# Scores of head pairs in two-bank PSUM tiles, with the softmax of a pair in single VectorE instructions

## The chip, the cores and the metric

The kernel runs on one core of one Trainium2 chip. The metric is the device time of one execution in microseconds (us). Before the change the median of 3 runs is 740.6 us (740.55 to 742.78). The profiled execution took 741.12 us, of which 739.3 us is the span, from the first to the last recorded instruction.

## The reference, cut to what matters

One inference step of a small decoder with model width 1024, for a prompt of 256 tokens and for 8 sample tokens with 256 cached positions each: an S5 (state-space) layer with a gated output, a squared-ReLU MLP, an attention layer, and a second MLP, all in float32. In the attention layer every query mixes three branches with gates: a compressed one, a selection one and a window one.

```
q  = rope(rms_norm(h @ w_q));  gates = sigmoid(h @ w_gate)      # 16 query heads of 64, 4 KV heads
p_c = masked_softmax(q @ kc);  p_s = masked_softmax(q @ ks);  p_w = masked_softmax(q @ kw)
o  = g0 * (p_c @ vc) + g1 * (p_s @ vs) + g2 * (p_w @ vw)
x  = x + o @ w_o
x  = x + square(relu(rms_norm(x) @ w_up)) @ w_down
```

With 256 tokens the selection takes every causal block, and the window of 512 covers the whole prompt. So the selection and the window branch of a head are two causal softmaxes over 256 keys, with different keys and values.

## The kernel before, in words

Prompt and sample tokens stand side by side as 264 columns (NT), features on the 128 partitions. A dense product splits a float32 weight tile into a rounded part and a rest (wsplit, L590 on ScalarE and L591 on VectorE), and makes three matmuls of each pair of tiles (mm3, L597 to L599).

The stages follow each other: the S5 layer to about 133 us, its gated product and the first MLP to 364, keys, values and queries to 441, the attention to 528, the output product to 554, the second MLP to the end. The S5 stage has an order written out by hand; the code of the other stages is written as generators, and the scheduler of the framework orders the instructions of each engine by when their tiles and buffers come free. So the number of PSUM buffers behind each tag is part of what sets the order.

PSUM has 8 banks of 2 KB a partition, 512 float32 each. The tags and their buffers are set at the end of the file: PSC (whole kernel) has fl=2 and tr=3; PSA (S5, gated product, first MLP) has mm=3; PSB (from then on) has sc=2 for scores and po=1 for attention outputs, and mm stands for the two fl banks there.

The prompt attention (prompt_attn) goes through 12 units (gp, rp, u). A unit is two heads, one of each of the KV groups 2gp and 2gp+1, whose keys lie on partitions 0 to 63 and 64 to 127. With u = 0 it is the first 128 queries of two heads for each group, with u = 1 or 2 the second 128 queries of one head each. In step i the code issues the scores of unit i, the softmax of unit i-1, and the transposes and value products of unit i-2.

- scores (L1181): two tiles of tag sc, one bank each. For u > 0 a product over 64 rows gives 512 columns of a head, selection and window side by side (L1195), and a product with a triangle constant adds the causal mask (L1198). For u = 0 the mask comes first (L1187), and then L1191, 256 columns a time.
- softmax (L1202): for each bank on its own a maximum on VectorE (L1212), one exponential on ScalarE for each row of scores (L1214, 4 or 2 a bank), and on VectorE the reciprocal, the gates (L1218) and the product (L1223). P has four buffers.
- transposed (L1227) brings P into key order by four transposes a bank (L1232), and values (L1244) multiplies with the values into the one po bank.

Beside the units runs other work, in two generators, side_a and side_b. The first has the rest of the second query group (q1: dense product, transposes L934, normalisation and rotary form from L987 on, transposes back L944 and copy L945) and the compressed branch of the second pair of groups; the second is the attention of the 8 sample tokens (sample_qk, sample_attn), which takes banks of tag mm. The tables SIDE and SIDB say how many steps of each are issued behind each unit, and Q1 how many steps of q1 come before the first unit. cmp_branch(0), the compressed branch of the first pair of groups, is issued before the first scores (products L1156).

Of the kernel before, what the change touches and what calls it, by code (L numbers as in the profile page):

```python
# [81 lines left out]
F32 = mybir.dt.float32  # L82
# [75 lines left out]
def s5_stage(K, filler):  # L158
# [183 lines left out]
    def chunk_in(h):  # L342
        St[h] = e8([128, 2, 16, 73], f"St{h}")
        for ri in range(2):
            S.activation(St[h][:, ri, :, 0:8], st[:, h, ri], AF.Copy, scale=1.0 - 2 * ri)
        for q0 in range(0, 8, 3):
            n = min(3, 8 - q0)
            pt = [ps("mm"), ps("tr")]
            for q in range(n):
                qq = q0 + q  # L350
                for ri in range(2):
                    o = 146 * q + 73 * ri
                    for b in range(2):
                        for a in range(2):
                            nc.tensor.matmul(pt[a][64 * b:64 * b + 64, o:o + 73],
                                             ET[h][64 * a:64 * a + 64, qq, ri, 64 * b:64 * b + 64],
                                             U[64 * a:64 * a + 64, h, qq, b], start=True, stop=True)
            for a in range(2):
                pv_ = pt[a][:, 0:146 * n].rearrange("p (q r n) -> p r q n", r=2, n=73)
                sl = slice(2 * q0 + a, 2 * (q0 + n), 2)  # L360
                S.activation(St[h][:, :, sl, 8:73], pv_[:, :, :, 8:73], AF.Copy)
                S.activation(bu[:, h, :, sl], pv_[:, :, :, 0:8], AF.Copy)
# [163 lines left out]
    pys = {}  # L526
# [14 lines left out]
    for ft in range(4, 8):  # L541
        pys[ft] = ps("mm" if ft < 7 else "tr")
        conv(ft, pys[ft])
# [152 lines left out]
PDP = ()  # L696
PDA = ()
# [60 lines left out]
def sample_compress(K):  # L758
# [27 lines left out]
    for s in range(2):  # L786
# [3 lines left out]
        pts = [K.ps("fl"), K.ps("fl")]  # L790
# [157 lines left out]
def kv_post(K, br):  # L948
# [9 lines left out]
    pk = token_major(K, "sc", kv[:, 0:2])  # L958
# [6 lines left out]
    pv = token_major(K, "sc", kv[:, 2:4])  # L965
# [118 lines left out]
def gates(K, xh, xl):  # L1084
# [11 lines left out]
    S.activation(g, g, AF.Sigmoid)  # L1096
    K.gp = at.tile([128, 2, 16, 3], F32, name="gp")
# [44 lines left out]
def prompt_attn(K, oh, ol, side):  # L1142
# [38 lines left out]
    def scores(gp, rp, u):  # L1181

        banks = [K.ps("sc"), K.ps("sc")]
# [16 lines left out]
        return banks  # L1200

    def softmax(gp, rp, u, banks):  # L1202
        n = 4 if u == 0 else 2
        L = 512 // n
        out = []
        for g2 in range(2):
            head = (2 * gp + g2) * 4 + 2 * rp + max(u - 1, 0)
            sv = banks[g2].rearrange("p (n k) -> p n k", n=n)
            nm = aa.tile([128, n], F32, tag="nm", name="nm", bufs=6)
            den = aa.tile([128, n], F32, tag="den", name="den", bufs=6)  # L1210
            P = aa.tile([128, 522], F32, tag="P", name="P", bufs=4)[:, 0:512].rearrange("p (n k) -> p n k", n=n)
            V.tensor_reduce(nm, sv, AX.X, ALU.max, negate=True)  # L1212
            for i in range(n):
                S.activation(P[:, i], sv[:, i], AF.Exp, bias=nm[:, i:i + 1], accum_out=den[:, i:i + 1])  # L1214
            V.reciprocal(den, den)
            g = K.gp[:, 0, head:head + 2, 1:3] if u == 0 else K.gp[:, 1, head:head + 1, 1:3]
            dv = den.rearrange("p (h b) -> p h b", b=2)
            V.tensor_tensor(dv, dv, g, ALU.mult)  # L1218
            if (u > 0, g2) in PDA:
                for i in range(n):  # L1220
                    S.activation(P[:, i], P[:, i], AF.Copy, scale=den[:, i:i + 1])
            else:
                (G if (u > 0, g2) in PDP else V).tensor_tensor(P, P, den.unsqueeze(2).to_broadcast([128, n, L]), ALU.mult)  # L1223
            out.append(P)
        return out

    def transposed(gp, rp, u, Ps, PTs):  # L1227
        for g2 in range(2):
            pt = K.ps("tr")
            Pf = Ps[g2].rearrange("p n k -> p (n k)")  # L1230
# [29 lines left out]
    cmp_branch(0)  # L1260
    for i in range(n + 2):
        if i < n:
            sc[i] = scores(*units[i])
        if 1 <= i <= n:
            sm[i - 1] = softmax(*units[i - 1], sc.pop(i - 1))
# [78 lines left out]
def sample_attn(K, oh, ol):  # L1344
# [6 lines left out]
    for bh in range(2):  # L1351
        p1, p2 = K.ps("mm"), K.ps("mm")
# [53 lines left out]
        pc = K.ps("mm")  # L1406
        nc.tensor.matmul(pc[:, 0:64], ptx[:, 0], K.vcs[:, bh], start=True, stop=True)
# [5 lines left out]
        V.tensor_tensor(o, o, pc[:, 0:64], ALU.add)  # L1413
# [34 lines left out]
def build(ctx, tc, A, O):  # L1448
# [13 lines left out]
    K.ps = lambda tag: pools[tag][0].tile([128, 512], F32, tag=pools[tag][2], name="ps_" + tag, bufs=pools[tag][1])  # L1462
# [63 lines left out]
    pools["mm"] = pools["fl"]  # L1526
    with ExitStack() as es:
# [59 lines left out]
        with ExitStack() as ek:  # L1587
# [15 lines left out]
            def side(i, cmp_branch):  # L1603
                if not steps:
                    steps.extend([side_a(cmp_branch), side_b()])
                for _ in range(SIDE[i]):
                    next(steps[0], None)
                for _ in range(SIDB[i]):
                    next(steps[1], None)
            prompt_attn(K, oh, ol, side)  # L1610
            for s in steps:
                for _ in s:
                    pass
        yh, yl = ft(F32R, "yh"), ft(F32R, "yl")
# [14 lines left out]
PSC = dict(fl=2, tr=3)  # L1629
PSA = dict(mm=3)  # L1630
PSB = dict(sc=2,po=1)
SIDE = (3,1,1,1,0,0,1,1,1,1,0,0,0,0)
SIDB = (1,2,2,2,2,2,2,2,0,0,0,0,0,0)
Q1 = 2
# [95 lines left out]
```

## Time and profile before

| | |
|---|---|
| Median of the runs | 740.6 us (740.55 to 742.78) |
| Profiled execution, its own time | 741.12 us |
| Its span | 739.3 us |
| PE (TensorE) busy | 700.2 us, 95% of the span, 6,214 matmuls |
| DVE (VectorE) busy | 531.7 us, 72% |
| ACT (ScalarE) busy | 404.6 us, 55% |
| POOL (GpSimd) busy | 74.8 us, 10% |
| Mean granted clock of TensorE | 0.975 of full speed |
| Chain that ended last | PE 83%, DVE 13%, ACT 2% |

PE is the matmul side of TensorE and PEld its weight loads, which run beside the matmuls. The granted clock is the TensorE clock as a share of 2.4 GHz. Matmuls are pipelined, and the ends of their records are modelled: a record's length holds latency too, so from one matmul to the next it is the distance of their starts that counts. The chain follows the work that ended last back to what released it, step by step.

### The profile page before, as it was taken

To read this page: it belongs to the slowest core of one execution; us is meant where nothing else is said; L and a number is where in the kernel's file an instruction comes from. 1 tells how busy PE (TensorE), PEld (TensorE's weight loads), DVE (VectorE), ACT (ScalarE), POOL (GpSimd) and SP (SyncE) were. 2 spreads that over 40 slices of the span, in tenths; PEclk is the share of its full clock that TensorE was granted. 3 is DMA by queue.
4 is the path that set the end of the run, shared out by engine and by line. 5 is a ranking of instruction groups with operands and counts; after the bars stand their busy time and mean duration, and the time that the engine had idled before them with its cause. 6 is when DMAs were issued, how large, how long until landed. Compare 5 with 4: busy or idle time off the path is not lost.

```text
span 739.3 us, 16322 instructions
## 1 busy us (share of the span) xinstructions
PE 700.2 (95%) x6214; PEld 650.7 (88%) x6214; DVE 531.7 (72%) x1209; ACT 404.6 (55%) x907; POOL 74.8 (10%) x127
## 2 busy tenths in 40 slices
PE   2789897999999999999998999999999999999997
PEld 2787777999999999999988984565899999999997
DVE  7899995978777766656677868887678777755553
ACT  3463532666666655445466575657466666644442
POOL 0000623111000000000002224110020000000000
PEclk9989897999999999999999996999999999999999
DMA  7342423686767758555555564100255555556551
GB/s 263 81 158 77 161 99 118 197 289 193 229 234 262 277 175 298 186 175 188 177 175 179 188 187 142 59 3 1 86 172 182 188 173 182 189 180 201 192 190 40
DMA packets 53328, 124.70 MB, mean 169 GB/s; under 512 B 6522, under 2 KB 26874, under 8 KB 52994
## 3 DMA queue, kind: packets, MB, share of 16 engines
q1 hardware_dynamic: 51714, 121.23, 49.9%
q10 hardware_dynamic: 1536, 2.42, 0.9%
q8 instruction: 49, 0.80, 0.5%
q14 instruction: 29, 0.24, 0.1%
HBM read 120.63 MB, written 7.18 MB: 173 GB/s over the span
## 4 chain that ended last, share of the span: by engine, by line
PE 83%; DVE 13%; ACT 2%; issue 1%; DMA 1%; SPq 0%; ACTq 0%; DVEq 0%
PE ps_mm L597 23%; PE ps_mm L598 22%; PE ps_mm L599 22%; PE ps_sc L1195 3%; PE ps_tr L296 2%; PE ps_tr L1232 2%; PE ps_po L1253 2%; DVE ca L431 1%; DVE St L434 1%; DVE St L433 1%; DVE cb L432 1%; DVE St L455 1%; DMA U<-x_chunks_in 1%; DVE big L454 1%; PE ps_sc L1198 1%
## 5 line engine op out<-in xcount | busy, mean ns | idle before, releaser
L591 DVE TENSOR_TENSOR wl<-raw,wh 128x512 fp32r<-128x512 f32 x344 | 241.1, 703 | 149.5 <-ACT wh L590 146.5
L590 ACT ACTIVATE wh<-raw 128x512 fp32r<-128x512 f32 x344 | 216.0, 631 | 210.7 <-PE ps_mm L598 157.8
L597 PE MATMUL ps_mm<-hh,wh 128*128 128x264 f32 x512 | 145.3, 284 | 0.0
L598 PE MATMUL ps_mm<-hl,wh 128*128 128x264 f32 x512 | 145.0, 283 | 0.0
L599 PE MATMUL ps_mm<-hh,wl 128*128 128x264 f32 x512 | 145.0, 283 | 0.0
L598 PEld LDWEIGHTS ps_mm<-hl,wh 128*128 128x128 f32 x512 | 96.5, 188 | 0.0
L597 PEld LDWEIGHTS ps_mm<-hh,wh 128*128 128x128 f32 x512 | 96.4, 188 | 0.0
L599 PEld LDWEIGHTS ps_mm<-hh,wl 128*128 128x128 f32 x512 | 96.0, 187 | 0.0
L598 PE MATMUL ps_mm<-yl,wh 128*128 128x264 f32 x256 | 72.9, 285 | 0.0
L597 PE MATMUL ps_mm<-yh,wh 128*128 128x264 f32 x256 | 72.6, 284 | 0.0
L597 PE MATMUL ps_mm<-xh,wh 128*128 128x264 f32 x256 | 72.6, 284 | 0.0
L599 PE MATMUL ps_mm<-yh,wl 128*128 128x264 f32 x256 | 72.5, 283 | 0.0
L598 PE MATMUL ps_mm<-xl,wh 128*128 128x264 f32 x256 | 72.4, 283 | 0.0
L599 PE MATMUL ps_mm<-xh,wl 128*128 128x264 f32 x256 | 72.3, 284 | 0.0
L597 PEld LDWEIGHTS ps_mm<-yh,wh 128*128 128x128 f32 x256 | 48.2, 188 | 0.0
L598 PEld LDWEIGHTS ps_mm<-xl,wh 128*128 128x128 f32 x256 | 48.2, 188 | 0.0
L597 PEld LDWEIGHTS ps_mm<-xh,wh 128*128 128x128 f32 x256 | 48.2, 188 | 0.0
L599 PEld LDWEIGHTS ps_mm<-yh,wl 128*128 128x128 f32 x256 | 48.2, 188 | 0.0
L598 PEld LDWEIGHTS ps_mm<-yl,wh 128*128 128x128 f32 x256 | 48.1, 188 | 0.0
L599 PEld LDWEIGHTS ps_mm<-xh,wl 128*128 128x128 f32 x256 | 47.9, 188 | 0.0
L628 POOL TENSOR_TENSOR nacc<-nacc,sq 128x264 f32<-128x264 f32 x21 | 16.9, 803 | 251.9 <-ACT sq L627 251.9
L598 PE MATMUL ps_mm<-gl,wh 128*128 128x264 f32 x128 | 36.6, 289 | 0.0
(424 smaller groups left out, 1482.3 us busy)
## 6 DMA issues: line engine op xcount, KB each, us to landing
raw<-w_up_in SPq DMA_DIRECT2D x64, 512.0 KB, 3.8
raw<-w_down_in SPq DMA_DIRECT2D x64, 512.0 KB, 3.6
raw<-s_w_glu_in SPq DMA_DIRECT2D x16, 512.0 KB, 4.8
w<-cmp_w_in SPq DMA_DIRECT2D x12, 512.0 KB, 4.5
raw<-w_kv_in SPq DMA_DIRECT2D x12, 512.0 KB, 3.5
blk<-cache_cmp_in SPq DMA_DIRECT2D x64, 64.0 KB, 1.9
raw<-w_q_in SPq DMA_DIRECT2D x8, 512.0 KB, 3.7
win_old_out<-cache_win_kv_in SPq DMA_DIRECT2D x8, 510.0 KB, 5.2
```

Source lines behind the costliest of these rows:

```text
L296: nc.tensor.matmul(pm[:, 0:73], sameT, sq[:, h, q, b], start=(h + q + b == 0), stop=(h + q + b == 9))
L431: TT(a, x, m(SR), ALU.mult)
L432: TT(b_, x[:, ::-1], m(SQ), ALU.mult)
L590: nc.scalar.activation(h[:, :, cols], src[:, c:c + 4], AF.Copy)
L591: nc.vector.tensor_tensor(l[:, :, cols], src[:, c:c + 4], h[:, :, cols].bitcast(F32), ALU.subtract)
L597: nc.tensor.matmul(out, wh, xh, start=start, stop=False)
L598: nc.tensor.matmul(out, wh, xl, start=False, stop=False)
L599: nc.tensor.matmul(out, wl, xh, start=False, stop=stop)
L628: nc.gpsimd.tensor_tensor(self.acc, self.acc, sq, ALU.add)
L1195: nc.tensor.matmul(banks[g2], K.QT[hs[g2], 4 * gp + 2 * rp + u - 1, 128:256], K.KTp[hs[g2], gp], start=True, stop=False)
L1232: nc.tensor.transpose(pt[:, 128 * j:128 * j + 128], Pf[:, 128 * j:128 * j + 128], K.ident)
L1253: nc.tensor.matmul(po[64 * g2:64 * g2 + 64, 128 * kt:256], K.Vp[:, kt, br, 64 * g:64 * g + 64], rhs, start=False, stop=(br == 1 and kt == 1))
```

## The change

PSUM tiles of a new tag s2 have 1,024 columns, two banks. A unit's scores stand in one such tile, each head in one bank of it. The softmax takes the pair in one maximum, one reciprocal, one product with the gates and one product with P, which is now one tile of 1,024 columns with two buffers. The exponentials stay one to a row of scores. The eight banks are dealt anew: PSC has fl=1 and tr=2, PSA has mm=4 and a bank fb, PSB has two s2 (four banks) and po=1. In the stages after the first MLP a product of tag mm takes in turn the fl bank and half of each s2 tile; during the attention it takes the fl bank alone.

Smaller edits: the keys' and values' transposes (token_major) go to tag tr; the S5 stage names its banks anew; the samples' scores take an s2 tile, and their compressed output (pc) shares the po bank; the gates get a one-element exponential (tle) behind their sigmoid; cmp_branch(0) is issued behind the first scores; and the tables SIDE, SIDB and Q1 have new numbers.

```diff
     S.activation(g, g, AF.Sigmoid)
+    S.activation(ak.tile([1, 1], F32, name="tle"), g[0:1, 0:1], AF.Exp)
...
-        banks = [K.ps("sc"), K.ps("sc")]
+        pair = K.ps("s2")
+        banks = [pair[:, 0:512], pair[:, 512:1024]]
...
     def softmax(gp, rp, u, banks):
         n = 4 if u == 0 else 2
...
+        sv = banks.rearrange("p (n k) -> p n k", n=2 * n)
+        nm = aa.tile([128, 2 * n], F32, tag="nm", name="nm", bufs=4)
+        den = aa.tile([128, 2 * n], F32, tag="den", name="den", bufs=4)
+        P = aa.tile([128, 1024], F32, tag="P", name="P", bufs=2)
+        Pv = P.rearrange("p (n k) -> p n k", n=2 * n)
+        V.tensor_reduce(nm, sv, AX.X, ALU.max, negate=True)
+        for i in range(2 * n):
+            S.activation(Pv[:, i], sv[:, i], AF.Exp, bias=nm[:, i:i + 1], accum_out=den[:, i:i + 1])
+        V.reciprocal(den, den)
...
+        V.tensor_tensor(dv, dv, g, ALU.mult)
+        V.tensor_tensor(Pv, Pv, den.unsqueeze(2).to_broadcast([128, 2 * n, 512 // n]), ALU.mult)
+        return P[:, 0:512], P[:, 512:1024]
...
-    cmp_branch(0)
     for i in range(n + 2):
         if i < n:
             sc[i] = scores(*units[i])
+        if i == 0:
+            cmp_branch(0)
...
-        p1, p2 = K.ps("mm"), K.ps("mm")
+        pair = K.ps("s2")
+        p1, p2 = pair[:, 0:512], pair[:, 512:1024]
...
+    K.mm = ["mm"]
+
+    def ps(tag):
+
+        if tag == "mm":
+            tag = K.mm[0]
+            K.mm.append(K.mm.pop(0))
+            if tag == "s2":
+                return ps(tag)[:, 0:512]
...
-    pools["mm"] = pools["fl"]
+    wide = ["fl", "s2", "s2"]
+    K.mm = list(wide)
...
+            K.mm = ["fl"]
             prompt_attn(K, oh, ol, side)
...
+            K.mm = list(wide)
...
-PSC = dict(fl=2, tr=3)
-PSA = dict(mm=3)
-PSB = dict(sc=2,po=1)
-SIDE = (3,1,1,1,0,0,1,1,1,1,0,0,0,0)
-SIDB = (1,2,2,2,2,2,2,2,0,0,0,0,0,0)
-Q1 = 2
+PSC = dict(fl=1, tr=2)
+PSA = dict(mm=4, fb=1)
+PSB = dict(s2=2, po=1)
+SIDE = (1,1,1,2,2,2,1,1,1,1,0,0,0,0)
+SIDB = (0,0,0,1,2,2,2,2,2,2,2,0,0,0)
+Q1 = 1
```

TensorE at the start of the prompt attention, before. The names are those of the code; qr is a query tile that is brought into token order, P the probabilities of a unit:

```order
L934 MATMUL ps_mm<-ident,qr_5939 128x128 x4
L1156 MATMUL ps_po<-kcb,QT 128x16 x8
L1300 MATMUL ps_mm<-ssq,cst 128x96
L1195 MATMUL ps_sc<-KTp,QT 128x512
L1198 MATMUL ps_sc<-triR,identR 128x2x128
L1195 MATMUL ps_sc<-KTp,QT 128x512
L1198 MATMUL ps_sc<-triR,identR 128x2x128
L1195 MATMUL ps_sc<-KTp,QT 128x512
L1198 MATMUL ps_sc<-triR,identR 128x2x128
L1232 MATMUL ps_tr<-ident,P 128x128 x4
L1195 MATMUL ps_sc<-KTp,QT 128x512
L1198 MATMUL ps_sc<-triR,identR 128x2x128
```

The same place after; the scores of three units, with the tiles ps_s_5998, ps_s_6070 and ps_s_6126, and other products between them:

```order
L932 MATMUL ps_tr<-ident,kv 128x128 x4
L1099 MATMUL ps_tr<-ident,gT 128x48 x2
L1191 MATMUL ps_s_5998<-KTp,QT 128x256 x4
L1195 MATMUL ps_s_6070<-KTp,QT 128x512 x2
L1198 MATMUL ps_s_6070<-triR,identR 128x2x128 x2
L1107 MATMUL ps_tr<-cst,glt 128x3
L972 MATMUL ps_tr<-ident,kv 8x128 x2
L942 MATMUL ps_fl<-ident,qn 128x128 x4
L1107 MATMUL ps_tr<-cst,glt 128x3
L1294 MATMUL ps_fl<-ssq,cst 128x96
L1195 MATMUL ps_s_6126<-KTp,QT 128x512 x2
L1198 MATMUL ps_s_6126<-triR,identR 128x2x128 x2
```

The two products L1195 of a unit and its two masks L1198 now stand next to each other, where they alternated. Work that was done before this place (the transposes of values and gates) now stands in it.

ScalarE at the same place, before; t is the square of a query tile, P the exponentials:

```order
L987 ACTIVATE t<-ps_mm 128x512
L1298 ACTIVATE ssq<-sK 128x96
L1214 ACT_TABLE_LOAD
L1214 ACTIVATE P,den<-ps_sc,nm 128x128 x8
L1214 ACTIVATE P,den<-ps_sc,nm 128x256 x4
```

And after:

```order
L985 ACTIVATE t<-ps_fl 128x512
L943 ACTIVATE KTp<-ps_tr 128x2x256
L965 ACTIVATE tm<-ps_tr,rt 128x256 x2
L1100 ACTIVATE gp<-ps_tr 128x96
L973 ACTIVATE vnew<-ps_tr,rt 8x256
L943 ACTIVATE QT<-ps_fl 128x512
L1109 ACTIVATE gs<-ps_tr 128x6
L1292 ACTIVATE ssq<-sK 128x96
L1211 ACTIVATE P,den<-ps_s_5998,nm 128x128 x8
L1211 ACTIVATE P,den<-ps_s_6070,nm 128x256 x4
```

The table load is gone from here, and between the last square of a query tile and the first exponential stand seven evictions, among them the copy of the last query tiles (QT).

## Rows read from the trace of the kernel before

**Rows 1.** Stages: stretch, length, busy PE, PEld, DVE, ACT, POOL, clock, DMA, GB/s.

```profile
178.00:364.10 186.10, 186.10 (x1540) 186.03 (x1539) 123.39 (x220) 106.46 (x213) 6.68 (x13) 1.00 0.67 221
441.40:462.90 21.50, 19.55 (x67) 11.23 (x66) 17.47 (x63) 13.11 (x48) 8.88 (x15) 0.68 0.46 146
462.90:523.10 60.20, 60.09 (x446) 35.58 (x444) 46.55 (x148) 37.03 (x152) 5.89 (x14) 1.00 0.06 19
```

**Rows 2.** The same view, the attention's first part split by the granted clock.

```profile
441.40:446.20 4.80, 2.85 (x21) 2.38 (x20) 4.04 (x12) 4.63 (x17) 0.53 (x1) 1.00 0.89 272
446.20:459.80 13.60, 13.60 (x31) 6.74 (x30) 10.79 (x47) 6.95 (x28) 7.30 (x13) 0.50 0.42 135
```

**Rows 3.** TensorE groups, 441.4 to 528.4: count, busy, mean ns, idle before.

```profile
L1195 PE MATMUL ps_sc<-KTp,QT 64*128 64x512 f32 x32 | 21.3, 751 | 1.7 <-ACT P L1214 1.6
L1191 PE MATMUL ps_sc<-KTp,QT 64*128 64x256 f32 x24 | 6.0, 417 | 0.0
```

**Rows 4.** Timeline of TensorE: start, length of the group, instruction, records.

```profile
435.21 1.13 PE L1191 MATMUL ps_sc<-KTp,QT 64*128 64x256 f32 x8
...
461.52 1.13 PE L1191 MATMUL ps_sc<-KTp,QT 64*128 64x256 f32 x4
...
465.92 1.12 PE L1195 MATMUL ps_sc<-KTp,QT 64*128 64x512 f32 x2
466.98 0.38 PE L1198 MATMUL ps_sc<-triR,identR 128*128 128x256 f32 x1
467.29 1.12 PE L1195 MATMUL ps_sc<-KTp,QT 64*128 64x512 f32 x2
468.34 0.39 PE L1198 MATMUL ps_sc<-triR,identR 128*128 128x256 f32 x1
468.57 0.60 PE L1232 MATMUL ps_tr<-ident,P 128*128 128x128 f32 x4
```

**Rows 5.** Timeline of all engines near 443 us; idle before in brackets.

```profile
441.87 1.93 PE L1156 MATMUL ps_po<-kcb,QT 128*128 128x16 f32 x16 [0.35 <-DVE vcm L1079]
...
442.83 1.28 ACT L1214 ACT_TABLE_LOAD   x1
...
444.13 0.37 ACT L1214 ACTIVATE P<-ps_sc,nm 128x128 f32<-128x128 f32 x1
...
445.51 0.38 ACT L1214 ACTIVATE P<-ps_sc,nm 128x128 f32<-128x128 f32 x1
...
445.69 1.63 PE L1195 MATMUL ps_sc<-KTp,QT 64*128 64x512 f32 x2 [1.60 <-ACT P L1214]
```

**Rows 6.** Timeline of TensorE where the compression tail stands.

```profile
133.71 0.27 PE L823 MATMUL ps_fl<-ident,kc 128*64 128x128 f32 x1 [0.52 <-DVE kc L755]
```

**Rows 7.** Groups of the query normalisation, from 436 or 441.4 to 528.4.

```profile
L987 ACT ACTIVATE t<-ps_mm 128x512 f32<-128x512 f32 x2 | 1.2, 595 | 0.2 <-PE ps_mm L934 0.2
L988 DVE TENSOR_REDUCE ss<-t 128x8 f32<-128x512 f32 x2 | 1.3, 672 | 0.0
L991 DVE TENSOR_TENSOR qn<-ps_mm,T0q 128x512 f32<-128x512 f32 x2 | 1.4, 676 | 0.0
L993 DVE TENSOR_TENSOR t<-ps_mm,T1q 128x256 f32<-128x256 f32 x4 | 1.5, 414 | 0.0
L133 DVE TENSOR_TENSOR rs<-rs 128x8 f32<-128x8 f32 x6 | 1.3, 215 | 0.0
L998 POOL TENSOR_TENSOR qn<-qn,ri 128x512 f32<-128x512 f32 x2 | 2.6, 1301 | 9.6 <-DVE den L1218 8.8 <-DVE ri L137 0.8
L945 ACT ACTIVATE QT<-ps_mm 128x512 f32<-128x512 f32 x2 | 1.2, 600 | 0.0
```

**Rows 8.** ScalarE group, 364.1 to 441.4, eviction of a query tile.

```profile
L1124 ACT ACTIVATE qr<-ps_mm 128x264 f32<-128x264 f32 x7 | 2.6, 375 | 0.0
```

**Rows 9.** VectorE: a group of the attention, and one instruction of the timeline.

```profile
L1212 DVE TENSOR_REDUCE nm<-ps_sc 128x2 f32<-128x512 f32 x16 | 11.0, 688 | 6.7 <-PE ps_sc L1198 6.7
...
379.51 1.26 DVE L925 TENSOR_TENSOR kv<-kv,rstd 128x1056 f32<-128x1056 f32 x1 [0.59 <-ACT rstd L904]
```

More of the change, by code (lines that the diff above doesn't have):

```diff
@@ L347, in chunk_in @@
             n = min(3, 8 - q0)
-            pt = [ps("mm"), ps("tr")]
+            pt = [ps("mm"), ps("mm")]
             for q in range(n):
@@ L541, in s5_stage @@
     for ft in range(4, 8):
-        pys[ft] = ps("mm" if ft < 7 else "tr")
+        pys[ft] = ps("mm")
         conv(ft, pys[ft])
@@ L695 @@
 NP = 'm'
-PDP = ()
-PDA = ()
 CPA = (0,)
@@ L789, in sample_compress @@
         yield
-        pts = [K.ps("fl"), K.ps("fl")]
+        pts = [K.ps("fl"), K.ps("fb")]
         for lc in range(4):
@@ L957, in kv_post @@
     tm = K.ak.tile([128, 2, 512], F32, tag="tmk", name="tm", bufs=2)
-    pk = token_major(K, "sc", kv[:, 0:2])
+    pk = token_major(K, "tr", kv[:, 0:2])
     G.tensor_copy(K.sK[:, 2 * br - 2:2 * br], kv[:, 0:2, 0:8])
@@ L964, in kv_post @@
         yield
-    pv = token_major(K, "sc", kv[:, 2:4])
+    pv = token_major(K, "tr", kv[:, 2:4])
     for qt in range(2):
@@ L1199, in scores @@
                                  K.triR.unsqueeze(1).to_broadcast([128, 2, 128]), start=False, stop=True)
-        return banks
+        return pair
     def softmax(gp, rp, u, banks):
         n = 4 if u == 0 else 2
[L1204 to L1224, printed above, removed]
@@ L1225, in softmax @@
-        return out
+        sv = banks.rearrange("p (n k) -> p n k", n=2 * n)
[6 more added lines that the diff above has]
+            S.activation(Pv[:, i], sv[:, i], AF.Exp, bias=nm[:, i:i + 1], accum_out=den[:, i:i + 1])
@@ L1227, in transposed @@
+        V.reciprocal(den, den)
+        head = 8 * gp + 2 * rp + max(u - 1, 0)
+        g = K.gp[:, min(u, 1)].rearrange("p (g h) b -> p g h b", h=4)[:, 2 * gp:2 * gp + 2, head % 4:head % 4 + n // 2, 1:3]
+        dv = den.rearrange("p (g h b) -> p g h b", g=2, b=2)
+        V.tensor_tensor(dv, dv, g, ALU.mult)
+        V.tensor_tensor(Pv, Pv, den.unsqueeze(2).to_broadcast([128, 2 * n, 512 // n]), ALU.mult)
+        return P[:, 0:512], P[:, 512:1024]
     def transposed(gp, rp, u, Ps, PTs):
@@ L1229, in transposed @@
             pt = K.ps("tr")
-            Pf = Ps[g2].rearrange("p n k -> p (n k)")
+            Pf = Ps[g2]
             for j in range(4):
@@ L1405, in sample_attn @@
                                      vr[bh][br][:, b4, pg], start=False, stop=(br == 1 and pg == 1))
-        pc = K.ps("mm")
-        nc.tensor.matmul(pc[:, 0:64], ptx[:, 0], K.vcs[:, bh], start=True, stop=True)
+        pc = po[:, 256:320]
+        nc.tensor.matmul(pc, ptx[:, 0], K.vcs[:, bh], start=True, stop=True)
         t = K.tmp.tile([128, NT], F32, tag="t", name="so")[:, 0:256].rearrange("p (g d) -> p g d", g=4)
@@ L1412, in sample_attn @@
         V.tensor_reduce(o, t.rearrange("p g d -> p d g"), AX.X, ALU.add)
-        V.tensor_tensor(o, o, pc[:, 0:64], ALU.add)
+        V.tensor_tensor(o, o, pc, ALU.add)
         yield
@@ L1461, in psum @@
             pools[tag] = pool, bufs[tag], tag
-    K.ps = lambda tag: pools[tag][0].tile([128, 512], F32, tag=pools[tag][2], name="ps_" + tag, bufs=pools[tag][1])
+    K.mm = ["mm"]
[5 more added lines that the diff above has]
+                return ps(tag)[:, 0:512]
+        pool, bufs, t = pools[tag]
+        return pool.tile([128, 1024 if tag == "s2" else 512], F32, tag=t, name="ps_" + tag, bufs=bufs)
+    K.ps = ps
     psum(ctx, "pc", PSC)
```

## The prediction

> **What bounds the kernel now.** I read the stages first (busy time by stretch), then the chain of waits, then the TensorE rows of the attention, then the waits inside it. In the dense stages TensorE is busy all the time: 1,540 matmuls start in 186.1 us, one every 0.12 us, at the full clock [rows 1]. Nothing but fewer matmuls shortens those, and the change removes none; more PSUM buffers there are worth nothing. The prompt attention, from 441.4 to about 528 us, is the other kind of stage: TensorE is busy 60.09 of 60.2 us in its second part, but not by work that has to take so long, and in its first part 13.6 us run at a granted clock of 0.50, the 1.2 GHz level [rows 1, 2]. DVE is busy 46.55 and ScalarE 37.03 of the same 60.2 us, so both come behind TensorE. What a change of TensorE's order in this stage gains is therefore real until DVE or a wait takes over.
>
> **The change part by part.** All sums go against the profiled execution: span 739.3, its own time 741.1 us. The 1.8 us around the span stay. The median of the runs is 740.6, so 0.5 us come off at the end.
>
> *Scores in pairs.* A unit is two heads of two KV groups. Its two score matmuls use rows 0 to 63 and rows 64 to 127 of the array. Before, the banks came free one at a time, and the scheduler put the causal mask (L1198) of the first between them. After, all 8 units with u > 0 issue L1195 twice in a row, then L1198 twice. What the neighbourhood is worth, the trace shows on L1191, the same product for u = 0: eight records on both halves, in turn, take 1.13 us (435.21), and four records on one half take 1.13 us too (461.52) [rows 4]. The two halves run side by side. One L1195 alone holds TensorE 1.05 us (465.92 to 466.98, 467.29 to 468.34; 32 records, 16 matmuls [rows 3, 4]). So 8 units x 1.05 = 8.4 us. Of the four units with u = 0, two are in pairs already; the unit at gp 1 becomes one, 1.06, and the one at rp 1 half, since eight transposes stand in its middle, 0.5 (24 records of L1191 in the stretch [rows 3]): 1.6 us. Each change between the two forms also costs: L1198 before L1195 takes 0.31 us (466.98 to 467.29), before a transpose 0.23 (468.34 to 468.57), so 0.09 rounded up [rows 4]; two changes less per unit, 8 x 2 x 0.09 = 1.4. Together 11.4 us at the full clock. Bounds: 1.4 if two 512-column products do not overlap, 11.4 if they do; I take 11.4, because the nearest row is the same line of work at 256 columns.
>
> *Waits that go.* TensorE waits 1.60 us at 445.69 for the first exponentials, which stood behind a table load of 1.28 us on ScalarE [rows 5]. The new one-element exponential in the gates loads that table earlier, under dense products: 1.6 us go. The compression tail moves out of the first dense stage into the MLP, and with it the 0.52 us at 133.71 [rows 6]; if its new place waits as long, that is nought.
>
> *Waits that come.* First, the pipeline's start. Two units' scores are issued, and the third needs the first pair of banks, which is released by all 8 exponentials of the first unit. In ScalarE's new order they stand behind the copy of QT, which needs the whole normalisation of the second query group: 0.60 (L987) + 0.67 + 0.68 + 2 x 0.41 on DVE + two small ones of 0.2 each + eleven rsqrt steps at 0.2 = 2.4, then 1.30 on GpSimd, four transposes 0.5, and the copy 0.60 = 8.0 us [rows 7]. Four exponentials end to start take 1.38 us (444.13 to 445.51), so 8 take 2.8 [rows 5]: 10.8 us in all. Beside it TensorE has L1156, 1.93, two units of scores, 1.13 + 1.12 + 0.5, and some 17 small products at 0.12, 2.0: 6.7 us [rows 1, 4, 5]. It waits 4.1 us; with the rsqrt on GpSimd, which the next product needs, I say 4.5. Second, the query tiles: three of them now follow each other in one bank, where two alternated; an eviction takes 0.38 us [rows 8] plus its hand-over, say 0.6, twice, 1.2. Third, all later uses of the single bank and of the two transpose banks where three were: by the order, most have other products between write and eviction; I give them 3.0. New waits 8.7 us. Bounds: 3, if the start alone waits and less than reckoned, and 22 (14 uses of the single bank, each at the 1.6 us of rows 5).
>
> *Clock.* Before, 13.6 us at the lower level cost half, 6.8 us, since TensorE was busy throughout; ahead of the fall it was busy 2.85 of 4.8 us [rows 2]. After, the start is at least as thin, so I expect the fall again, but 3.9 us of the stretch lie under the waits above: (13.6 - 3.9) / 2 = 4.9, gain 1.9 us. Bounds: a gain of 6.8, if it does not fall, and a loss of 6.8, for one more such stretch.
> The Trainium skill ("TensorE: Matmul & The Clock Gate", "A second HAM failure mode: psum-queue depth-cycling") says that a kernel that cycles through PSUM banks with small idles between groups makes the clock swing between its levels. From 462.9 us on the present kernel does cycle through banks and keeps 1.00 [rows 1], so here the rule has not bitten; by it the change, with more idles, would lose the further stretch, which is the third rival below.
>
> *Softmax in single instructions.* A reduction over 512 takes 0.69 us; over 1,056 elements DVE took 1.26 [rows 9], so over 1,024 about 1.23 against 2 x 0.69. Per unit DVE loses some 0.5 us of work with the product and the small ones, nine units in the second part, 4.5 of its 46.55 us. Nothing of it is on the path, so I cost it at nothing; what hides it is TensorE. The first exponential starts 0.5 us later, covered by the other unit's work except at the start, where the 4.5 us above have it.
> The Trainium skill ("TensorEngine Tiling (Array Packing)", "PSUM Bottleneck") warns that array tiles speed up TensorE, not the emptying of PSUM. Here DVE's 42 us against some 52 us left to TensorE agree with it in kind: the margin is 10 us, and by the rule the best case below is less likely than the wait sum alone makes it.
>
> *The rest.* In the recurrent stage only bank names change on TensorE and DVE up to its last scan, which DVE paces: nought, 0.5 us either way. On SyncE the value loads of the samples now stand behind the store of the new keys; by the order some 25 us of products lie between that store and their first use: nought.
>
> Sum: -11.4 - 1.6 - 0.5 + 8.7 - 1.9 = -6.7; 741.1 - 6.7 = 734.4, and against the median 733.9, so 734 us.
>
> **The rivals.**
> 1. *Better:* the clock stays up and the later waits do not come: 734 - 4.9 - 3.0 = 726. For it, TensorE has dense products until just before; against it, the fall in the same place now, and DVE's narrow margin.
> 2. *Slower, the single bank:* during the attention all sample products, two transposes of queries and their evictions share one bank, 14 uses. If each holds TensorE 1.6 us, 22.4 us come in place of the 4.2 that I gave them: 734 + 18.2 = 752. It decides from 10.9 / 14 = 0.8 us a use. Against it: before, with two banks, only one wait of 1.6 us is seen in the whole stage.
> 3. *Clock:* one more stretch at half speed, 6.8 us: 741, no change.
> 4. *The pairs do not overlap* at 512 columns: 8.4 + 1.6 come back, 744, slower. The L1191 rows speak against it.
>
> **How the numbers follow.** Chances: forecast 0.53 (its own range 729 to 739), better 0.20, clock 0.13, single bank 0.09, no overlap 0.05. About 0.3%, 2.2 us, is what a measurement of this kernel can tell from no change: faster means below 738.4, slower above 742.8. Faster is most of the forecast and the better case, 0.71; same is its tail and most of the clock rival, 0.13; slower is the rest, 0.16. The range 726 to 742 leaves out the single bank, the missing overlap and a little below 726.
>
> **What would show it.** In the new profile: the second of two L1195 starts within 0.02 us of the first, and a pair ends after about 1.1 us; no table load within the attention; TensorE idle for some 3 to 5 us before the third unit's scores, put down to exponentials; a stretch of 0.50 near 445 us, not longer than 13.6 us; dense stages unchanged to 0.5 us; TensorE busy less than its stage, with DVE above 80% of it. Pairs of 2.1 us, or waits on the single bank beyond 11 us in all, would make the prediction wrong.

## The result, and the profile after

The changed kernel takes 748.95 us (median of 4 runs, 747.49 to 750.17) against 740.58 for the kernel before beside it (737.57 to 742.78): a ratio of 1.0115, interval 1.0075 to 1.0155. It is slower by 1.15%, where 734 us, faster by 0.9%, was forecast. Its profiled execution took 749.07 us, with a span of 747.2: 7.9 us more than before.

Stage lengths come first: busy time by stretch, in the columns of [rows 1]. For the kernel before, the two stretches are the recurrent stage up to its first gated product, and all of keys, values, queries and attention:

```profile
0.00:116.30 116.30, 88.33 (x1226) 80.28 (x1226) 103.90 (x262) 50.41 (x94) 24.39 (x47) 0.92 0.44 143
358.80:548.80 190.00, 185.25 (x1384) 144.84 (x1383) 144.16 (x415) 117.64 (x342) 36.54 (x53) 0.96 0.37 121
```

The same view of the changed kernel, then its attention split by the granted clock:

```profile
0.00:118.20 118.20, 92.93 (x1226) 82.87 (x1226) 103.23 (x260) 50.35 (x94) 19.08 (x37) 0.90 0.43 141
362.00:556.70 194.70, 181.32 (x1384) 146.80 (x1383) 139.61 (x366) 115.50 (x343) 34.76 (x53) 0.94 0.36 118
...
392.45:395.86 3.41, 2.92 (x13) 2.92 (x14) 3.41 (x11) 1.31 (x4) 0.00 (x0) 0.50 0.45 154
...
444.40:447.06 2.66, 1.33 (x10) 0.76 (x10) 2.56 (x10) 1.78 (x5) 0.20 (x1) 1.00 0.55 166
447.06:453.89 6.83, 6.82 (x33) 6.50 (x35) 5.36 (x18) 1.57 (x4) 3.15 (x3) 0.50 0.39 131
453.89:460.71 6.82, 3.56 (x22) 2.21 (x19) 3.76 (x10) 3.43 (x17) 1.08 (x2) 1.00 0.21 79
460.71:474.37 13.66, 12.87 (x40) 7.46 (x40) 9.19 (x24) 8.29 (x37) 6.63 (x14) 0.50 0.00 0
474.37:527.20 52.83, 50.31 (x418) 31.33 (x416) 39.33 (x105) 32.98 (x140) 5.76 (x13) 1.00 0.27 81
```

Attention with its dense neighbours grew from 190.0 to 194.7 us on the same 1,384 matmuls. TensorE's idle time (stretch less busy) grew from 4.75 to 13.4 us, so its busy time fell, 185.25 to 181.32. Part of that busy time ran at the 1.2 GHz level: 13.6 us before [rows 2], 2.92 + 6.82 + 12.87 = 22.6 after. Taking half of it off leaves the work, as it would be at the full clock: 178.4 before, 170.0 after. So, for the stage: work -8.4, idle +8.6, half speed +4.5 us, together +4.7. In these two profiles the recurrent stage ends 1.9 us later (118.2 for 116.3), at a granted clock of 0.90 where it was 0.92, and the first MLP, where the compression tail now stands, grew by 1.4. The gated product and the second MLP kept their lengths.

Groups of TensorE and VectorE in the attention, after (columns of [rows 3, 9]):

```profile
L1195 PE MATMUL ps_s<-KTp,QT 64*128 64x512 f32 x32 | 10.7, 747 | 3.4 <-ACT P L1211 3.4
L1209 DVE TENSOR_REDUCE nm<-ps_s 128x4 f32<-128x1024 f32 x8 | 9.7, 1213 | 1.4 <-PE ps_s L1198 1.3
```

The timeline of TensorE at a unit of the second query group, to set beside [rows 4]:

```profile
482.27 1.13 PE L1195 MATMUL ps_s<-KTp,QT 64*128 64x512 f32 x4
483.32 0.50 PE L1198 MATMUL ps_s<-triR,identR 128*128 128x256 f32 x2
483.76 1.51 PE L1246 MATMUL ps_po<-PT,Vp 128*64 128x256 f32 x14
```

Four records, both heads, take 1.05 us from start to start, the time that two took. The same 32 records fell from 21.3 [rows 3] to 10.7 us of busy time, in a stage that ran longer at half speed.

Waits of TensorE in keys to output product, after (engine, line, waited for: us in total, times, longest):

```profile
PE ps_s L1195 <- ACT P L1211: 3.4, 1, 3.4
PE ps_fl L942 <- POOL qn L996: 1.8, 1, 1.8
PE ps_s L598 <- DVE ql L610: 1.7, 1, 1.7
PE ps_tr L942 <- POOL qn L996: 1.6, 1, 1.6
PE ps_s L597 <- ACT qh L609: 1.2, 1, 1.2
PE ps_fl L597 <- ACT qr L1123: 0.9, 1, 0.9
```

One of them stood in the kernel before as well:

```profile
PE ps_mm L598 <- DVE ql L610: 1.8, 1, 1.8
```

There is no new wait of 8 us to point at. The pipeline's start costs 3.4 us, and the other new ones are a handful of waits between 0.5 and 1.8, each for a step on another engine.

All engines where the first exponentials stand, after, against [rows 5]:

```profile
455.97 0.28 DVE L1105 TENSOR_TENSOR glt<-gT,cst 48x128 f32<-48x128 f32 x1 [3.21 <-PE ps_tr L1107]
...
456.72 0.60 ACT L943 ACTIVATE QT<-ps_fl 128x512 f32<-128x512 f32 x1
...
457.09 0.29 DVE L1157 TENSOR_TENSOR cS<-ps_po,cst 128x128 f32<-128x128 f32 x1 [0.83 <-PE ps_tr L1107]
...
457.30 2.35 DVE L1209 TENSOR_REDUCE nm<-ps_s 128x8 f32<-128x1024 f32 x2
...
458.55 0.37 ACT L1211 ACTIVATE P<-ps_s,nm 128x128 f32<-128x128 f32 x1 [0.99 <-DVE nm L1209]
...
461.50 1.23 PE L1195 MATMUL ps_s<-KTp,QT 64*128 64x512 f32 x2 [3.43 <-ACT P L1211]
```

The table load of [rows 5] is gone. The third unit's scores wait for the first unit's eight exponentials. Those stand behind the copy of QT, but they waited 0.99 us more for the first maximum (L1209). It stood on VectorE behind a product of the gates (glt, L1105) and a step of the compressed branch (cS, L1157), before which VectorE was idle for 3.21 and 0.83 us, both put down to TensorE's small gate products (L1107).

**Time at half speed.** Executions of one kernel differ more than one profile can show: 97 runs of the kernel before, on five chips, lie between 736 and 754 us, and 17 on a single chip spread as far. Twice (1 - granted clock) times the span gives a run's time at the lower level. Within the kernels, over all runs of this study, the time rises by 0.41 us for each us at half speed, which accounts for 88% of the differences between runs of one kernel. The means from here on leave out the slow runs, those over 1.5% above the fastest of their kernel (13 of the 97). The kernel before has 35.8 us at half speed in the mean, the changed one 52.7. Set to an equal 34 us, the means are 739.7 and 741.1. So of 8.4 us between the means (740.5 and 748.9) some 1.4 are order and waits, and the other 7.0 go with the clock. "At equal clock" below means this comparison. It is a regression, not an experiment.

### The profile page after: what moved, and what is told of

The parts are those of the page before. It is cut to its first block, busy times and chain, and to the rows that moved or that the text cites. A ratio compares the mean times of both kernels' runs of the same rounds, so it can differ in the third digit from the quotient of the medians.

```text
span 747.2 us, 16264 instructions
## 1 busy us (share of the span) xinstructions
PE 701.2 (94%) x6214; PEld 655.7 (88%) x6214; DVE 526.8 (71%) x1161; ACT 402.6 (54%) x908; POOL 70.7 (9%) x127
## 4 chain that ended last, share of the span: by engine, by line
PE 86%; DVE 5%; ACT 3%; SPq 2%; issue 2%; DMA 1%; POOL 0%; ACTq 0%; DVEq 0%; POOLq 0%
PE ps_mm L597 10%; PE ps_mm L598 10%; PE ps_mm L599 10%; PE ps_s L598 8%; PE ps_s L597 8%; PE ps_s L599 8%; PE ps_fl L597 4%; PE ps_fl L598 4%; PE ps_fl L599 4%; SPq L769 2%; PE ps_tr L296 2%; PE ps_fl L793 2%; PE ps_po L1246 2%; PE ps_fb L793 2%; PE ps_tr L1225 1%
## 5 line engine op out<-in xcount | busy, mean ns | idle before, releaser
L597 PE MATMUL ps_mm<-hh,wh 128*128 128x264 f32 x256 | 72.6, 284 | 0.0
L597 PE MATMUL ps_mm<-xh,wh 128*128 128x264 f32 x256 | 72.6, 284 | 0.0
L598 PE MATMUL ps_mm<-hl,wh 128*128 128x264 f32 x256 | 72.5, 283 | 0.0
L599 PE MATMUL ps_mm<-hh,wl 128*128 128x264 f32 x256 | 72.5, 283 | 0.0
L597 PE MATMUL ps_s<-hh,wh 128*128 128x264 f32 x192 | 54.5, 284 | 0.0
L598 PE MATMUL ps_s<-hl,wh 128*128 128x264 f32 x192 | 54.4, 283 | 0.0
L599 PE MATMUL ps_s<-hh,wl 128*128 128x264 f32 x192 | 54.4, 283 | 0.0
L597 PEld LDWEIGHTS ps_mm<-xh,wh 128*128 128x128 f32 x256 | 48.2, 188 | 0.0
L598 PEld LDWEIGHTS ps_mm<-hl,wh 128*128 128x128 f32 x256 | 48.2, 188 | 0.0
L597 PEld LDWEIGHTS ps_mm<-hh,wh 128*128 128x128 f32 x256 | 48.2, 188 | 0.0
L599 PEld LDWEIGHTS ps_mm<-hh,wl 128*128 128x128 f32 x256 | 48.0, 187 | 0.0
L598 PE MATMUL ps_s<-yl,wh 128*128 128x264 f32 x168 | 47.8, 285 | 0.0
L599 PE MATMUL ps_s<-yh,wl 128*128 128x264 f32 x168 | 47.6, 284 | 0.0
L597 PE MATMUL ps_s<-yh,wh 128*128 128x264 f32 x168 | 47.6, 283 | 0.0
L597 PE MATMUL ps_mm<-gh,wh 128*128 128x264 f32 x128 | 36.7, 290 | 0.0
```

Source lines behind the costliest of these rows:

```text
L597: nc.tensor.matmul(out, wh, xh, start=start, stop=False)
L598: nc.tensor.matmul(out, wh, xl, start=False, stop=False)
L599: nc.tensor.matmul(out, wl, xh, start=False, stop=stop)
```

## The experiments

The first theory was that the lost time lies in the start of the attention, its wait and the thin stretches around it, plus a late recurrent stage. The rivals were: the pairs or the single softmax gain nothing, the tables SIDE, SIDB and Q1 put the work in a bad place, or the single bank is the bottleneck. Ratios are to the kernel before on the same chip. The experiments ran on five chips, so two of them are compared by these ratios or at equal clock. "On e1" means that the first edit below is in as well.

**Do the pairs and the single softmax gain?** In e7 the mask is issued between the two products; in e8 the softmax goes bank by bank, as before.

```diff
e7:
-            for g2 in range(2):
e8:
-        V.tensor_reduce(nm, sv, AX.X, ALU.max, negate=True)
...
+        for g2 in range(2):
...
+            V.tensor_reduce(nq, sv, AX.X, ALU.max, negate=True)
```

> The changed kernel, with the causal mask of the first head issued between the two products of a unit with u > 0, so that the eight pairs L1195 no longer stand side by side. Theory: a pair saves 1.05 us and two changes of form, 8 x 1.2 = 9.8 us at the full clock, and TensorE bounds the attention after its start: about 757 us. Rival: after the change VectorE or ScalarE bounds the units, and TensorE's saving was already lost in waits: 751 us or less.

> The changed kernel, with the softmax again bank by bank (two maxima, reciprocals and products a unit), on the same two-bank tiles. Theory: the single instructions are worth nothing on the path, since VectorE has 10 us of slack, and the split gives the first exponentials 0.5 us earlier and lets the first transposes start on one half: 745 to 749 us. Rival: VectorE is near its bound in the attention, and 0.5 us more a unit shows, 12 x 0.5 = 6 us: 755 us.

e7: 762.07 us, ratio 1.0274 (1.0209 to 1.0339), some 12 us slower than the change by the ratios; 8.7 at equal clock. The forecast of 757 us left out the clock: e7 has 62 us at half speed in the mean, the change 53. TensorE's timeline of e7:

```profile
491.08 1.12 PE L1195 MATMUL ps_s<-KTp,QT 64*128 64x512 f32 x2
492.13 0.38 PE L1197 MATMUL ps_s<-triR,identR 128*128 128x256 f32 x1
492.44 1.12 PE L1195 MATMUL ps_s<-KTp,QT 64*128 64x512 f32 x2
493.50 0.38 PE L1197 MATMUL ps_s<-triR,identR 128*128 128x256 f32 x1
493.81 1.51 PE L1245 MATMUL ps_po<-PT,Vp 128*64 128x256 f32 x14
```

From the first product to the value products behind both masks it is 2.73 us (491.08 to 493.81), in the change 1.49 (482.27 to 483.76). Over the whole attention, by the distances of starts and halved where the clock was 0.50, the scores and masks hold TensorE 9.8 us longer in e7 than in the change; 9.8 was forecast. The pairs are real, and of the size forecast. e8: 748.43, ratio 1.0092 (1.0053 to 1.0132), no different from the change in time. At equal clock it is 2.2 us slower, but it had 9 us less at half speed, so the single softmax gains little, if anything, in the end.

**Is it the two-bank tile by itself, or the tables?** e3 puts one two-bank tile into the kernel before, which leaves its other banks as they were; the transposes of keys and values, which stood on the score banks, go to tag tr, as in the change. e4 is the change with the old tables.

```diff
e3 (on before):
-    pk = token_major(K, "sc", kv[:, 0:2])
+    pk = token_major(K, "tr", kv[:, 0:2])
...
-    pv = token_major(K, "sc", kv[:, 2:4])
+    pv = token_major(K, "tr", kv[:, 2:4])
...
-        banks = [K.ps("sc"), K.ps("sc")]
+        pair = K.ps("s2")
+        banks = [pair[:, 0:512], pair[:, 512:1024]]
...
-PSB = dict(sc=2,po=1)
+PSB = dict(s2=1,po=1)
e4 (on after):
+SIDE = (3,1,1,1,0,0,1,1,1,1,0,0,0,0)
+SIDB = (1,2,2,2,2,2,2,2,0,0,0,0,0,0)
+Q1 = 2
```

> The kernel before, with one two-bank tile for the scores of a unit in place of two one-bank tiles: the same number of banks, softmax still bank by bank, old tables. The two products L1195 of a unit then stand side by side. Theory: this side-by-side placing is the whole gain of the change and is worth 8 to 10 us of TensorE; the next unit's scores now wait for all exponentials of the unit before, a cycle of about 1.5 + 1.4 + 1.8 = 4.7 us beside 5.9 us of other TensorE work a unit, so most of it is hidden: 733 to 736 us. Rival: one tile makes scores and softmax take turns and each unit waits 1 us or more: 741 us or above.

> The changed kernel with SIDE, SIDB and Q1 of the kernel before. The exponentials of the first unit no longer stand behind the second query group's normalisation. Theory: the thin start of the attention is a matter of the pipeline filling, since the transposes of the first unit must still wait for maximum, exponentials and product (about 1.3 + 2.8 + 1.7 us); TensorE waits 3 to 5 us as now and the time stays at 747 to 751 us. Rival: the tables make the start thin; then the wait of 3.4 us and one half-speed stretch go, 742 us.

e3: 755.78, ratio 1.021 (1.0175 to 1.0246). A clear miss. With one tile the scores of only one unit can stand in PSUM, and TensorE waits at the transposes for that unit's softmax. Idle time in keys to attention was 24.7 us. The largest waits:

```profile
PE ps_tr L1233 <- DVE P L1224: 7.1, 4, 3.9
PE ps_mm L1301 <- ACT ssq L1299: 3.5, 1, 3.5
```

e4: 752.48, ratio 1.0174 (1.0133 to 1.0215), with 26.0 us idle, above what its theory and its rival gave. The old tables are worse under the new banks (5.9 us at equal clock), so the new ones are not the cause. Pairs need two two-bank tiles, which means four of eight banks.

**The banks of the recurrent stage.** e1 gives the stage's second transposing bank another tag. e2 gives the kernel before the naming of the change.

```diff
e1 (on after):
-            pt = [ps("mm"), ps("mm")]
+            pt = [ps("mm"), ps("tr" if q0 < 6 else "fb")]
e2 (on before):
-            pt = [ps("mm"), ps("tr")]
+            pt = [ps("mm"), ps("mm")]
...
-        pys[ft] = ps("mm" if ft < 7 else "tr")
+        pys[ft] = ps("mm")
...
-PSC = dict(fl=2, tr=3)
-PSA = dict(mm=3)
-PSB = dict(sc=2,po=1)
+PSC = dict(fl=2)
+PSA = dict(mm=4, tr=2)
+PSB = dict(sc=2,po=1,tr=3)
```

> The changed kernel, with one edit: the state-input products of the recurrent stage (L355) take their second bank from another tag again, so that three groups can be in flight where two can. Theory: with two in flight TensorE waits for evictions at 46 to 48 us, the clock falls at 51 us, the compression products and the page loads behind them come 7 us later, and the last output products of the stage come 3.3 us later. So the first gated product should start at about 116.3 us (118.2 in the changed kernel, 116.3 in the kernel before) and the time should fall by 1.9 us, to about 747. Rival: the fall of the clock at 51 us comes wherever it likes, and the first gated product stays at 118 us, time 749.

> The kernel before, with the recurrent stage's banks of the changed kernel alone (four mm, two tr, the state-input products in pairs of mm); the attention keeps its banks and its order. Theory: the loss of the recurrent stage comes with this edit, first gated product at about 118.2 us and 742.5 us in all. Rival: no change, 740.6 us.

e1: 746.18, ratio 1.0101 (1.0069 to 1.0133). That is near its theory's 747, but by the ratios only 1 us better than the change, well within the intervals. e2: 744.01, ratio 1.0049 (1.0018 to 1.008), so the new names alone cost some 3 to 4 us. At equal clock neither differs from its parent (741.0 against 741.1; 739.8 against 739.7): what the names cost comes as time at half speed, 41.8 us in e2 beside 33.0 in before on the same chip. Where that time arises is not settled, and the start of the first gated product, by which both theories are put, can't tell. It is 114.8 us in e1's profile and 119.1 in e2's, but 118.9 in e3's, with the old names, and 113.4 in e8's, with the new ones. It goes with the half-speed time before it, which was 16.9, 23.9, 23.9 and 17.1 us in these four. The profiles of e2 and of the change show TensorE waiting over 4 us for a weight transfer of the compression, here e2's wait:

```profile
PE ps_fl L795 <- DMA w<-cmp_w_in: 4.9, 1, 4.9
```

But e3's profile, with the old names, has the same wait at 3.7 us. It differs between executions, and one profile of each can't tie it to the names.

**The table load.** e5 is the kernel before with the one-element exponential alone.

```diff
+    S.activation(ak.tile([1, 1], F32, name="tle"), g[0:1, 0:1], AF.Exp)
```

> The kernel before, with the one-element exponential of the changed kernel behind the sigmoid of the gates, and nothing else. Theory: the table load of 1.28 us leaves the start of the attention, the 1.6 us wait of TensorE at 445.7 us goes, and with a fuller start the half-speed stretch of 13.6 us gets shorter or stays away: at equal clock 1.6 us less, in all 1.6 to 8 us less than before, so 732 to 738 us beside 739 to 740. Rival: the first exponentials wait for maxima and copies anyway; no change.

e5: 738.96, ratio 0.9989 (0.9951 to 1.0028). The wait of 1.60 us [rows 5] is gone from its profile, and idle time in keys to attention fell from 4.75 to 3.8 us, but a gain can't be told from none. At equal clock it is 0.7 us, where 1.6 was forecast.

**Does the start's thin stretch pull the clock down?** e6 (on e1) puts three products of 512 columns, which nobody reads, before the third unit's scores. e10 does the like in the recurrent stage of before, e11 does that with e5's edit.

```diff
e6:
+        if i == 2:
+            warm = K.ps("tr")
+            for j in range(WARM):
+                nc.tensor.matmul(warm[0:6], ...)
e10, e11 (e11 with e5's line as well):
+    warm = ps("fl")
+    for j in range(5):
+        nc.tensor.matmul(warm, ident, ...)
```

> The changed kernel with the recurrent stage's banks of the first experiment (746 us), and three added products of 512 columns, whose result nobody reads, on TensorE where it waits 3.4 us before the third unit's scores. It does more work and computes the same. Theory: the fall of the clock behind that wait is what the wait costs most; with TensorE busy there the stretch of 13.7 us at half speed gets shorter or goes, and the time falls by 3 to 6 us, to 740 to 743 us. Rival: the clock falls because of the thin stretch from 434 to 447 us, or the waits are lost at full clock as well; then no change or 1 us more.

> The kernel before, with five added products of 512 columns, whose result nobody reads, in the recurrent stage, where TensorE waits 5.4 us for VectorE at 34 to 39.5 us and the clock falls at 36.6 us. Theory: with TensorE busy there the clock stays up; less time at half speed in this stage, and the time falls by 1 to 3 us, to 737 to 739 us. Rival: VectorE paces this stage and the clock is of no account in it: no change, 740 us.

> The kernel before, with the added products of the tenth experiment and the early exponential of the fifth, which took 2 us off the mean. If both are worth what their theories say, 735 to 737 us; if neither is, 740 us.

e6: 748.47, ratio 1.0103 (1.0047 to 1.016), no gain over e1, where 3 to 6 us were forecast. The stretches of e6 by clock:

```profile
448.00:454.80 6.80, 6.80 (x28) 4.89 (x27) 4.21 (x16) 1.57 (x4) 2.92 (x3) 0.50 0.42 152
454.80:475.30 20.50, 16.79 (x90) 9.12 (x89) 16.02 (x38) 15.47 (x69) 5.11 (x12) 1.00 0.12 34
475.30:482.10 6.80, 6.80 (x34) 4.37 (x37) 2.97 (x7) 2.00 (x8) 2.92 (x12) 0.50 0.21 61
```

The clock stayed at 2.4 GHz over the start, where the change fell after 6.8 us, and fell 20.5 us later; TensorE was idle for 3.7 us in between. The scores' wait at the start shrank from 3.43 to 0.93 us, but the fill also changed the order behind it, and a new wait of 3.3 us stands at the samples' scores. Half-speed time came down to 39.9 us in the mean, but at equal clock the kernel is 5.4 us slower than e1. e10: 745.37, 1.0051 (1.0016 to 1.0086), slower where 1 to 3 us of gain were forecast, by 3.1 us at equal clock. In its profile the first half-speed stretch of before, at 36.6 us, is absent; one twice as long begins at 47.6 us, and its mean half-speed time is not lower, 38.5 us. e11: 742.60, 1.0031 (0.9988 to 1.0074), no gain either; its first stretch begins at 48.7 us. In the fifteen profiles without this fill it begins between 31.8 and 38.7. Filling a gap moves a fall; it did not buy time.

**Do single repairs of the waits help?** All are on e1. e9 takes only the first two units' softmax bank by bank. e12 puts the keys' and values' transposes on the score banks, e13 the gates' as well. e14 takes the sample norm's two products off the single bank. e15 has the edits of e12 and e14 and computes the sample norm's root on VectorE instead of GpSimd.

```diff
e9:
+        if (gp, rp) == (0, 0) and u < 2:
...
+            for g2 in range(2):
e12, e13, e15:
-    pk = token_major(K, "tr", kv[:, 0:2])
+    pk = token_major(K, "mm", kv[:, 0:2])
...
-    pv = token_major(K, "tr", kv[:, 2:4])
+    pv = token_major(K, "mm", kv[:, 2:4])
e13, twice:
-    pg = K.ps("tr")
+    pg = K.ps("mm")
e14, e15, twice:
-    pt = K.ps("mm")
+    pt = K.ps("tr")
e15:
-    if 1:
+    if 0:
```

> The changed kernel with the recurrent stage's banks of the first experiment, and the softmax bank by bank for the first two units alone; the other ten keep the single instructions. Softmax by bank in all units was 2 us slower at equal clock but spent 9 us less at half speed. Theory: the start of the attention is where the clock is lost, since the first exponentials wait for a maximum over both banks and the first transposes for a product over both; so two units are enough: half-speed time as with softmax by bank (about 37 us in all with the better recurrent stage), no loss later, 741 to 743 us. Rival: the time at half speed comes from all units alike; then 745 to 747 us.

> The changed kernel with the recurrent stage's banks of the first experiment, and the transposes of keys and values (token_major, 16 products) on the mm rotation, which has the still empty score tiles, in place of the two tr banks. In the kernel before they stood on the empty score banks too. By the order the first units' scores then stand ahead of the last dense query products. Theory: what thins the start of the attention is the two tr banks, on which the transposes of keys, values, gates and queries queue up; with dense products beside the first exponentials the wait of 3.4 us goes, and the half-speed stretches at the start get shorter: 736 to 741 us (746 without the edit). Rival: the start is bound by the chain maximum, exponentials, product, and waits as long in another place: 745 us.

> As the twelfth, with the two small products of the gates (L1099, L1107) on the mm rotation too. The maximum of the first unit, which waits in the changed kernel behind the gates' products on VectorE, then comes earlier still. Theory: 734 to 740 us, faster than both kernels. Rival: as in the twelfth, 745 us.

> The changed kernel with the recurrent stage's banks of the first experiment, and the two products of the samples' normalisation (L1294, L1307) on the two transpose banks in place of the single mm bank. The single bank is then free for the second query group between them, and by the order its transposes move ahead. Theory: the single bank ties the queries to the samples' normalisation (some 6 to 10 us from L1294 to L1307), and TensorE has nothing else beside the first exponentials; freed, the start waits 2 to 3 us less and some of the time at half speed goes: 740 to 743 us (746 without). Rival: only the chain maximum, exponentials, product counts; 745 us.

> As the twelfth (keys' and values' transposes on the empty score tiles, 760 us with a new wait of 6.8 us for the samples' normalisation), with the samples' two products on the transpose banks and their inverse root on VectorE in place of twelve steps on GpSimd that took 5 us. Theory: the new wait of the twelfth run was this chain, which TensorE meets because its other work was moved ahead; with the chain shorter and off the single bank that wait falls to 2 us or less, and what the twelfth meant to gain shows: 738 to 745 us. Rival: the waits move on to the next chain, as in the ninth and the twelfth: above 748 us.

e9: 744.75, ratio 1.0037 (1.0001 to 1.0074), not the 741 to 743 of its theory. The start's wait of 3.4 us left the scores and came back, at the same size, at the transposes of P:

```profile
PE ps_tr L1243 <- DVE P L1220: 3.4, 1, 3.4
```

e12: 760.34, 1.0219 (1.0159 to 1.028); e13: 755.03, 1.0153 (1.0086 to 1.0221); e14: 755.88, 1.0218 (1.017 to 1.0266). All three missed. In e12 the first units' scores start without a wait, and other chains are late instead:

```profile
PE ps_fl L1307 <- DVE ssq L1305: 6.8, 1, 6.8
PE ps_tr L1225 <- DVE rs L128: 4.1, 1, 4.1
```

The first is the sample norm. The timeline of GpSimd in e12 shows the chain that precedes it, 12 small dependent steps in 5.1 us, of which these are the first and the last:

```profile
470.02 0.34 POOL L1279 TENSOR_TENSOR rs<-rs 128x96 f32<-128x96 f32 x1 [6.93 <-DVE rs L1277]
...
474.71 0.39 POOL L1282 TENSOR_TENSOR sri<-rs,rs 128x96 f32<-128x96 f32 x1
```

e15 takes that chain off GpSimd: 744.62, 1.0057 (1.0024 to 1.009), within its forecast, some 12 us faster than e12 by the ratios, and still not faster than before. At equal clock e9 and e15 are the best of the changed kernels, 740.5 and 740.6, beside 739.7 before. Its waits show the next chain in line, the compressed branch's softmax:

```profile
PE ps_po L1176 <- DVE cS L1173: 4.2, 1, 4.2
PE ps_fl L597 <- ACT qr L1123: 2.8, 1, 2.8
PE ps_tr L1225 <- DVE P L1217: 1.7, 1, 1.7
```

Idle time in keys to attention was 15.1 us in e15. In all eleven profiles that bind four banks to scores (the change, e1, e4, e6 to e9, e12 to e15) it lay between 13.4 and 26.0; with two single banks (the kernel before, e2, e5, e10, e11) it lay between 3.8 and 5.9. TensorE's work in the same stages, at the full clock, goes by the pairs instead: 169.1 to 174.1 us in the profiles with pairs (e3 is one of them), 177.9 to 179.8 without (e7 is one of them). That is what the runs show in common. No run varies the number of banks alone: the eleven also share the two-bank tile and the later place of cmp_branch(0), and e3, with one two-bank tile on two banks, has 24.7 us idle. So the banks are the likely cause of the waits, not a shown one. Each edit also moved the scheduler's order elsewhere, so no single repair is a clean measurement of one wait, and whether some other order of the changed kernel has less idle time stays open.

## Why the prediction was wrong

*Step by step.* The terms of the forecast against the stages of the profile:

| Term | Forecast, us | Measured, us |
|---|---|---|
| TensorE's work in the attention (pairs) | -11.4 | -8.4 |
| Waits in these stages, gone and new | +7.1 | +8.6 |
| Clock in these stages | -1.9 | +4.5 |
| Other stages | -0.5 | +3.2 |
| Sum | -6.7 | +7.9 |

The step that failed most is the clock: "I expect the fall again, but 3.9 us of the stretch lie under the waits", a gain of 1.9, where these stages lost 4.5. The forecast kept the length of the one stretch that was there, 13.6 us, and laid part of the waits inside it, with a 3.9 that it does not work out. The profile shows three stretches, 3.41 + 6.83 + 13.66 = 23.9 us, with 1.3 us of idle time in them. The 3.43 us at the pipeline's start lie ahead of the last fall, at the full clock, but for 0.8. The waits make thin stretches of their own: TensorE was busy 1.33 of 2.66 us ahead of the fall at 447.1, and 3.56 of 6.82 us ahead of the one at 460.7. So a wait was paid for as idle time, and half speed followed it. That they come together is seen in the profile. That the wait brings the fall on is not shown: e6 kept the clock up at this place by filling it, but the fall came later, and no time was saved.

One pair of profiles does not fix the 4.5. The half-speed time in these stages is 10.2 to 23.9 us in the five profiles with two single score banks, 17.1 to 37.5 in the eleven with four bound. The runs settle the sign: 35.8 us in the mean before, 52.7 after, and 45.5 in e1, with the old names in the recurrent stage, beside 33.0 in before on its chip. The third rival, one more stretch, would have made this term -1.9 + 6.8 = +4.9, near the 4.5; it had a chance of 0.13, and its time of 741 us failed by the other terms.

The clock is not all of the miss. Without that term the forecast is -4.8 us, and at equal clock the runs show +1.4. These 6 us, beside some 9 for the clock (-1.9 forecast, +7.0 by the regression), lie in the next three terms, so the kernel would not have been faster at the old clock either.

*The pairs* were right in mechanism and in size: counted as for e7, scores and masks hold TensorE 11.0 us less than before, where 11.4 was forecast. The stages' work fell by only 8.4, because other products took 2.6 us more, 1.1 of it the value products; no run shows why.

*The waits* were right at the start (4.5 forecast, 3.43 measured), though the path went through VectorE's gates as well as the copy of QT. The later ones were too small: 4.2 forecast, 6.8 measured (13.4 - 3.4 idle now, 4.75 - 1.6 before). The single bank, the second rival, is not seen as their cause: direct waits of a later query tile on it come to 0.9 us (L597). What the sum left out are the waits on steps in other engines (GpSimd's qn 1.8 + 1.6, qh 1.2). That less other work can be issued ahead of them, with two fewer banks for transposes, queries and samples, fits the profiles but was not tested by itself.

*Other stages* were costed at a gain of 0.5. The recurrent stage took 1.9 us more in this pair of profiles; e2's runs show that new bank names there are not free, but its end moves by more than that between profiles, so the 1.9 is not shown to be theirs. The wait of 0.52 us at the compression tail [rows 6] is gone, but the gated product is no shorter for it, and the MLP that the tail moved into grew by 1.4 us, 0.8 of it the tail's eight products.

*Right:* the table load leaves the attention, a pair starts together and ends after 1.05 us, the second MLP keeps its 190.5 us. *Softmax:* 1.21 us for a maximum over 1,024 was forecast at 1.23, but VectorE stood at 74% from 474 to 527 us (39.33 of 52.83), not above 80%: there it was not what held the stage back. Ahead of the first fall it was nearly full (2.56 of 2.66 us from 444.40).

## What to carry to other kernels

Count the banks that a change binds, and look at every chain that used those banks to run ahead. Here 8.7 us of faster matmuls were given back as waits of 0.5 to 3.4 us on chains through other engines, and in the runs tried, filling or freeing one brought up the next. Where a change makes a stage thinner, price the clock as well as the idle time, and compare kernels at equal granted clock before explaining a per cent. In a scheduled program a small edit reorders what is far from it, so an ablation is read from its trace, not from its time alone.

## What the runs showed of the hardware

Runs of the kernel before spread from 736 to 754 us, on a single chip too, and their time at half speed from 21 to 77 us; over all kernels 0.41 us of time for each of these is close to the half that a busy TensorE would lose. Work put into one gap (e6, e10, e11) moved such a stretch to another place and did not shorten the run. Two products on the two row halves of the array share it fully at 512 columns: 1.05 us for both, as for one.
